# Forced orders where stages hand over, four modulation steps moved, unread matmuls in the routing, and a head scale on VectorE

## The chip, the cores and the metric

The kernel runs on one core of a Trainium2 chip. A core has five engines with a queue of instructions each: TensorE (PE: matmuls, transposes), VectorE (DVE), ScalarE (ACT), GpSimd (POOL) and SyncE (SP, which here only issues DMAs). Each works through its own queue in order; semaphores make one wait for another. The metric is device microseconds (us) of one execution; smaller is better.

## The reference

Two transformer blocks of two layers each, on 256 tokens of width 1024. What matters here is the end of the first block's layers (an mLSTM branch) and the second block.

```python
def _layer(...):                                   # first block, twice
    h_lat = _rms_norm(h_lf + flip(h_lb), g_hd)     # mLSTM heads: 4 of 64, each with its own norm
    y_c = sigmoid(co) * h_lat * silu(cz)
    x = x + gt * (concatenate([y_a, y_b, y_c]) @ w_out)

def second_block(x, c, ...):
    ada_in = silu(c)
    for i in range(2):
        mod = (ada_in @ w_ada[i] + b_ada[i]).reshape(b, 6, d)
        sh_m, sc_m, g_m, sh_f, sc_f, g_f = the six of mod
        hm = rmsnorm(x, norm_mix[i]) * (1 + sc_m) + sh_m
        if i == 0: y = dilated_mixer(hm, ...)
        else:      y = forgetting_mixer(hm, b_w_in, ...)      # FoX
        x = x + g_m * y
        hf = rmsnorm(x, norm_ffn[i]) * (1 + sc_f) + sh_f
        x = x + g_f * hierarchical_moe(hf, ...)
    return x

def hierarchical_moe(h, ...):      # top-1 of 4 groups, then top-2 of 4 experts in it
    ...                            # gates: (tokens, 16), two entries of a row are not zero
    hid = silu(t @ w_gate[e]) * (t @ w_up[e])
    y = sum over e of gates[:, e] * (hid @ w_down[e])
```

## The kernel before

It is written with a framework that keeps one list of instructions for each engine and orders it at build time; tiles come from pools with fixed numbers of buffers (four of `raw`, two of `big`, 1 MB each), and an instruction waits until the buffer that it takes is free. `tc.issue_after(ins)` holds what is issued under it behind `ins` on that engine's list. Tokens are two tiles T of 128; the 1024 columns of a result are two halves n.

The helpers `mm`, `tr`, `act`, `tt`, `ts`, `stt` (lines 281 to 302) issue one instruction each, so most rows of the profile have one of these lines. Matmuls of large weights are done three times in f16, with a weight or activation split in a high and a low part (`wh`, `wl`; `split_w`, line 457: ScalarE makes `wh` from a `raw` tile, VectorE `wl`). `proj` (line 502) is one such projection; between its steps it runs pieces of other work (`settle`, `tick`).

Modulation: `ada` (line 517) is a generator of eight steps for two of the six vectors; a step loads 1 MB of `w_ada` into a `raw` tile and does four fp32 matmuls with 32 output rows (`ps_ad<-raw,cz`; eight records in the trace). `tick(n, a)` takes `a` steps of the queue `adaq`. For layer 1 the vectors of its expert stage ("nf") are queued in `run2` (line 1428) and taken in FoX.

mLSTM: at the end of a tile `head_rstd` makes the head norm `hr` on GpSimd (line 333), and `head_scale` multiplies `yc` by it, on GpSimd too (line 733); TensorE then transposes `yc`. There are six such tiles.

A layer of the second block: `mixer(i)` (line 1451) does the dilated mixer (i=0) or FoX (i=1) and the output projection. After the last projection of a token tile, `post` (line 1478) adds the residual, squares, takes `rstd2`, transposes x (`x_T`), makes the rows `nhl` in two f16 parts (`split_x`: `hi` on ScalarE; `lo` of T=0 on GpSimd by way of `xn`, of T=1 on VectorE) and runs the `router`: logits by TensorE, a copy `lt`, comparisons `df` and the choice `kb` on VectorE. `place(T)` counts the chosen tokens with a matmul on `kb`, `onehot` makes selection matrices OH, `gather0(T)` gathers the first expert pair's rows with 16 matmuls.

`moe(i)` (line 1955) handles 16 experts in eight pairs P: `gate_up(P)` (16 fp32 matmuls, 32 records), `mt` and `mh` (silu times up; ScalarE and VectorE), two transposes and the copy `mhT`, `down(P, n)` for both halves (with an eviction into `oh`, high part on ScalarE, low on VectorE), and `scatter(P)`, eight f16 matmuls that add the pair's rows to four PSUM banks Y. The loop issues gate_up one pair ahead and scatter one pair behind:

```python
            if P < 7:
                gate_up(P + 1)
            ...                                  # transposes of mh, mhT
            if P:
                scatter(P - 1, range(2))
            ohs[P] = self.k4h("oh")
            for n in range(2):
                down(P, n, hT)
        scatter(7, range(2))
```

Then, for each half and tile, the residual: `rsd` (Y times the gate, VectorE) and an addition to x (GpSimd for n=0, VectorE for n=1). Behind it stands the store of the output in layer 1; in layer 0 the squares, the norm `xn`, and in FoX the transposes of `xn`, their modulation (`nv`) and the first projection. FoX (line 1711) first loads the small gate weights `wfr` and fetches and converts the first unit of `b_w_in` in eight pieces.

## Time and profile before

| | |
|---|---|
| median of three runs | 1301.38 us (1296.94 to 1303.22) |
| the profiled execution | 1301.36 us |
| its span, first to last instruction | 1299.2 us |
| mean granted TensorE clock | 0.978 of full speed |
| busy: PE, DVE, ACT, POOL | 1207.5, 772.2, 628.1, 235.2 us |
| HBM read | 288.80 MB, 224 GB/s over the span |

Stages, in us of the span: first block 0 to 550, dilated mixer to 853, first routing to 885, experts of layer 0 to 1002, handover to 1015, FoX to 1143, second routing to 1176, experts of layer 1 to 1291, last residual and store to 1299. A row of a timeline gives the start and length of one or several alike instructions, and in brackets how long the engine sat idle before and whose result ended that. An fp32 matmul has two records. The granted clock is a share of full speed: TensorE runs at one of two levels, 2.4 and 1.2 GHz, and a stretch's number is their mean.

### The profile page before, as it was taken

What the parts mean: (1) busy time and instruction counts of PE and PEld (TensorE: products, weight loads), DVE (VectorE), ACT (ScalarE), POOL (GpSimd) and SP (SyncE); (2) the same over time, 40 slices, a digit from 0 to 9 for tenths busy, and PEclk for the clock granted to TensorE, in tenths of its full rate; (3) what the DMA queues carried; (4) which work ended last, traced back from release to release, by engine and by line L of the source; (5) the groups of instructions that cost most, each with busy time, mean ns of one, the idle gap of its engine ahead of it and who ended that gap; (6) DMA issues with size and microseconds to landing.
All of it is one profiled execution on the core that took longest, in us unless ns stands there. A gap on an engine that the chain in (4) does not pass through costs nothing. (4 is left out here: it accounts for less than half of the span.)

```text
span 1299.2 us, 21044 instructions
## 1 busy us (share of the span) xinstructions
PE 1207.5 (93%) x8064; PEld 574.7 (44%) x8064; DVE 772.2 (59%) x1787; ACT 628.1 (48%) x1373; POOL 235.2 (18%) x254
## 2 busy tenths in 40 slices
PE   6889999989999999899999999979997899979997
PEld 3434544444444544344555555445432445545432
DVE  3776655685567667866778767754213586654213
ACT  3535554444545545666667776533112556533111
POOL 1112000121230001251353235010000413010000
PEclk9999999999999999999999999989999899979999
DMA  9743456244474474587544455867897686617895
GB/s 364 262 163 130 164 194 223 78 162 149 147 275 145 147 259 155 177 311 306 193 162 163 166 190 197 276 259 262 332 399 320 242 309 227 228 49 277 337 398 201
DMA packets 51133, 292.34 MB, mean 225 GB/s; under 512 B 5962, under 2 KB 6218, under 8 KB 24660
## 3 DMA queue, kind: packets, MB, share of 16 engines
q1 hardware_dynamic: 48292, 281.56, 58.7%
q0 software_dynamic: 2736, 9.39, 2.3%
q8 instruction: 65, 1.06, 0.3%
q14 instruction: 40, 0.33, 0.1%
HBM read 288.80 MB, written 2.13 MB: 224 GB/s over the span
## 5 line engine op out<-in xcount | busy, mean ns | idle before, releaser
L298 PE MATMUL ps_mm<-wh,x 128*128 128x512 f16 (+1 forms) x1120 | 381.0, 379 | 5.3 <-DVE x L717 2.0
L298 PEld LDWEIGHTS <-x 128*128 128x128 f16 (+1 forms) x2344 | 189.6, 98 | 245.6 <-issue 92.7
L298 PE MATMUL ps_mm<-wl,x 128*128 128x512 f16 (+1 forms) x736 | 277.1, 377 | 0.0
L459 DVE SCALAR_TENSOR_TENSOR wl<-raw,wh 128x1024 f16<-128x1024 f32 (+2 forms) x188 | 223.0, 1213 | 58.2 <-ACT wh L282 57.8
L282 ACT ACTIVATE wh<-raw 128x1024 f16<-128x1024 f32 (+2 forms) x188 | 183.1, 1015 | 62.6 <-PE ps_mm L298 56.5
L298 PE MATMUL ps_mm<-wh,y 128*128 128x512 f16 (+1 forms) x480 | 174.5, 376 | 0.5 <-DVE y L285 0.3
L298 PE MATMUL ps_ad<-raw,cz 128*32 128x512 f32 (+1 forms) x640 | 112.3, 577 | 13.9 <-DMA raw<-in_w_ada 13.8
L332 POOL TENSOR_SCALAR hss<-hss 128x8 f32<-128x8 f32 (+2 forms) x58 | 20.8, 359 | 446.8 <-DVE hss L726 433.0
L333 POOL TENSOR_TENSOR hr<-hss,nhalf 128x8 f32<-128x8 f32 (+2 forms) x58 | 90.8, 1566 | 4.8
L298 PEld LDWEIGHTS <-y 128*128 128x128 f16 x560 | 54.0, 100 | 60.6 <-issue 13.8
L293 DVE SCALAR_TENSOR_TENSOR oh<-ps_tr,ka,oh 128x512 f16<-128x512 f32 x32 | 24.0, 751 | 78.9 <-ACT oh L282 78.6
L282 ACT ACTIVATE e<-e,ka 128x128 f32<-128x128 f32 (+1 forms) x128 | 56.6, 443 | 24.5 <-DVE ka L1581 24.5
L302 PE MATMUL ps_tr<-consts,e 128*128 128x128 f32 x352 | 59.3, 280 | 1.3 <-DVE qk L293 0.4
L298 PE MATMUL ps_mm<-wh,big 128*128 128x512 f16 x192 | 58.1, 379 | 0.2 <-DVE big L293 0.2
L302 PEld LDWEIGHTS ps_tr<-consts,e 128*128 128x128 f32 x352 | 40.9, 141 | 29.1 <-issue 5.3
L282 ACT ACTIVATE oh<-ps_tr,ka 128x512 f16<-128x512 f32 x32 | 22.0, 687 | 54.5 <-PE ps_tr L298 54.5
L285 DVE TENSOR_TENSOR e2l<-ps_tr,e2h 128x384 f16<-128x384 f32 x64 | 34.1, 554 | 23.1 <-ACT e2h L282 22.1
L282 ACT ACTIVATE e<-ps_s,mx 128x512 f32<-128x512 f32 (+1 forms) x48 | 29.2, 612 | 34.4 <-DVE mx L1020 34.4
L285 DVE TENSOR_TENSOR el<-ps_tr,eh 128x512 f16<-128x512 f32 (+1 forms) x48 | 28.1, 598 | 27.4 <-ACT eh L282 27.1
L298 PEld LDWEIGHTS ps_ad<-raw,cz 128*32 128x32 f32 x640 | 21.2, 111 | 49.1 <-issue 36.5
L282 ACT ACTIVATE e2h<-ps_tr 128x384 f16<-128x384 f32 x64 | 30.0, 481 | 26.5 <-PE ps_o L298 14.5
L298 PEld LDWEIGHTS <-big 128*128 128x128 f16 x288 | 28.1, 98 | 32.5 <-DVE big L293 0.3
(377 smaller groups left out, 1983.8 us busy)
## 6 DMA issues: line engine op xcount, KB each, us to landing
raw<-in_w_ada SPq DMA_DIRECT2D x48, 1024.0 KB
raw<-in_a_w_in SPq DMA_DIRECT2D x36, 1024.0 KB
x<-in_w_gu SPq DMA_DIRECT2D x64, 512.0 KB
...
```

The costliest lines, as they stand in the source:

```text
L282: return self.nc.scalar.activation(out, in_, func, **kw)
L285: return self.nc.vector.tensor_tensor(out, a, b, op=op)
L293: return self.nc.vector.scalar_tensor_tensor(out, a, s, b, op0=op0, op1=op1)
L298: return self.nc.tensor.matmul(out, lhsT, rhs, start=start, stop=stop, **kw)
L302: return self.nc.tensor.transpose(out, in_, self.C("ident")[:n, :n])
L332: self.nc.gpsimd.tensor_scalar(in_, in_, eps, None, op0=OP.add)
L333: self.nc.gpsimd.tensor_tensor(out, in_, self.nhalf.to_broadcast(list(in_.shape)), op=OP.pow)
L459: (on or self.nc.vector).scalar_tensor_tensor(wl, raw, WS, wh, op0=OP.mult, op1=OP.subtract)
```

## The change

At the end of the mLSTM, `yc` is multiplied on VectorE. In the routing, the low part of the first tile's rows is made on VectorE too; `gather0(0)` moves behind the second tile's router, goes through the high parts first, and is followed by five matmuls whose result nobody reads; seven more stand behind the last projection; the second tile's low part is made behind its one-hot. In the experts, scatter(6) is held behind gate_up(7), one half ahead of the transposes of `mh` and one behind; the residual of half 0 is written between the two halves of scatter(7). In layer 0 the first FoX weight is fetched in P=6 and converted in P=7, four of the eight "nf" modulation steps are held behind scatter(7), with two `raw` and two `big` tiles, and the transposes of FoX's norm are held behind the last of these.

The core of the diff:

```diff
 helpers
     def mm(self, out, lhsT, rhs, start, stop, **kw):
-        return self.nc.tensor.matmul(out, lhsT, rhs, start=start, stop=stop, **kw)
+        i = self.nc.tensor.matmul(out, lhsT, rhs, start=start, stop=stop, **kw)
+        self.last_mm = i.ins
+        return i
+    def warm(self, n):
+        p = self.ps("mm").rearrange("p (a n) -> p a n", a=4)
+        for _ in range(n):
+            self.mm(p, self.identh, self.identh[:, None, :].to_broadcast([128, 4, 128]), True, True)
     def ada(...)
-            raw = self.raw()
+            raw = self.adaraw.popleft()() if self.adaraw else self.raw()
 mLSTM, end of a tile
-            self.head_scale(yc.rearrange("p (h d) -> p h d", d=64), yc.rearrange("p (h d) -> p h d", d=64),
-                            r[:, :, None].to_broadcast([128, 4, 64]), 4)
+            yv = yc.rearrange("p (h d) -> p h d", d=64)
+            self.tt(yv, yv, r[:, :, None].to_broadcast([128, 4, 64]), OP.mult)
 run2
-            else:
-                self.adaq.append(self.ada_feat(1, 1, 3, "nf", st["f", 1]))
 mixer, norm(T)
-            self.mod_T(self.xn[T], mods, xT, T)
+            with self.tc.issue_after(self.ada_last):
+                self.mod_T(self.xn[T], mods, xT, T)
 mixer, post(p, T, n, hf)
             self.resid(self.x[T][:, c], p, gb[n])
+            if hf and T and n:
+                self.warm(7)
...
                         self.place(T)
                         self.onehot(0, T, 0)
-                        yield 0.5
-                        self.gather0(T)
 fox
+        W[0] = self.W0
         wr = self.w1("wfr", (8, 16))
         nc.sync.dma_start(wr.rearrange("p k n -> p (k n)"), self.ap["b_w_f"])
-        W[0] = self.conv(self.fetch(units[0]), 1)
 split_x
-        if T == 0:
-            xn = self.k4("xn")
-            self.nc.gpsimd.tensor_scalar(xn, x, r, None, op0=OP.mult)
-            self.nc.gpsimd.tensor_tensor(lo, xn, hi, op=OP.subtract)
-        else:
-            self.stt(lo, x, r, hi, OP.mult, OP.subtract)
+        if T == 0:
+            self.split_lo(T, r)
+    def split_lo(self, T, r):
+        hi, lo = self.nhl[T]
+        self.stt(lo, self.x[T], r, hi, OP.mult, OP.subtract)
 gather0
-        for k in range(8):
-            for a in range(2):
+        for a in range(2):
+            for k in range(8):
 moe, ahead of the experts
-        self.place(1)
-        self.onehot(0, 1, 0)
+        with tc.issue_after(self.last_mm):
+            self.gather0(0)
+            self.warm(5)
+        with tc.issue_after(self.last_mm):
+            self.place(1)
+        oh = self.onehot(0, 1, 0)
+        with tc.issue_after(oh.ins):
+            self.split_lo(1, self.rx[:, 1:2])
         self.gather0(1)
 moe, scatter
-                        Y[T, n] = self.ps({(0, 0): "s", (0, 1): "s", (1, 0): "o", (1, 1): "ad"}[T, n])
+                        Y[T, n] = self.ps({(0, 0): "ad", (0, 1): "s", (1, 0): "o", (1, 1): "s"}[T, n])
 moe, the loop over P
             if P < 7:
-                gate_up(P + 1)
+                up_last = gate_up(P + 1)
...
+            if P == 7:
+                with tc.issue_after(up_last):
+                    scatter(P - 1, (0,))
             (transposes of mh, copy mhT)
-            if P:
+            if P == 6 and i == 0:
+                raws = self.fetch(ap["b_w_in"][0])
+            if P == 7 and i == 0:
+                self.W0 = self.conv(raws, 1)
+            if P == 7:
+                with tc.issue_after(up_last):
+                    scatter(P - 1, (1,))
+            elif P:
                 scatter(P - 1, range(2))
             (both halves of down(P))
-        scatter(7, range(2))
         self.xn = {}
-        (the residual, for n, for T: resid, square, normed or the store)
+        scatter(7, (0,))
+        close(0)
+        ins = scatter(7, (1,))
+        close(1)
+        if i == 0:
+            self.adaq.append(self.ada_feat(1, 1, 3, "nf", st["f", 1]))
+            self.adaraw.extend([self.raw, self.raw] + 2 * [lambda: self.big(F32, (4, 512))])
+            with tc.issue_after(ins):
+                self.tick(0, 4)
+            self.ada_last = self.last_mm
+        def close(n):
+            for T in range(2):
+                (the same residual for one n: resid, square, normed or the store)
```

What the orders become. TensorE at the end of layer 0: the last matmuls of scatter(7), the norm's transposes, the first projection. Before:

```order
L298 LDWEIGHTS OHT
L298 MATMUL ps_s<-oh,OHT 128x512
L298 LDWEIGHTS OHT
L298 MATMUL ps_ad<-oh,OHT 128x512
L302 MATMUL ps_tr<-consts,xn 128x128 x12
L298 LDWEIGHTS x_10884
L298 MATMUL ps_mm<-wh,x_10884 128x512
```

And now:

```order
L299 LDWEIGHTS OHT
L299 MATMUL ps_s<-oh,OHT 128x512
L299 MATMUL ps_ad<-raw,cz 32x512 x8
L299 MATMUL ps_ad<-big,cz 32x512 x8
L311 MATMUL ps_tr<-consts,xn 128x128 x12
L299 LDWEIGHTS x_10945
L299 MATMUL ps_mm<-wh,x_10945 128x512
```

Two groups of eight fp32 matmuls (four modulation steps) stand between scatter(7) and the transposes.

VectorE at the same place: evictions `oh`, residual products `rsd`, additions to `xin`, FoX weight halves `wl`, the norm's `ss` and `xn`. Before:

```order
L293 SCALAR_TENSOR_TENSOR oh<-ps_tr,ka,oh 128x512 x2
L285 TENSOR_TENSOR rsd<-ps_s,gate 128x512
L285 TENSOR_TENSOR rsd<-ps_o,gate 128x512
L285 TENSOR_TENSOR rsd<-ps_s,gate 128x512
L285 TENSOR_TENSOR rsd<-ps_ad,gate 128x512
L738 TENSOR_TENSOR xin<-xin,rsd 128x512 x2
L459 SCALAR_TENSOR_TENSOR wl<-raw,wh 128x512
L293 SCALAR_TENSOR_TENSOR ss<-ssq 128x1
L459 SCALAR_TENSOR_TENSOR wl<-raw,wh 128x512
L289 TENSOR_SCALAR xn<-xin,rs 128x512
L293 SCALAR_TENSOR_TENSOR ss<-ssq 128x1
L459 SCALAR_TENSOR_TENSOR wl<-raw,wh 128x512
```

Now:

```order
L294 SCALAR_TENSOR_TENSOR oh<-ps_tr,ka,oh 128x512
L468 SCALAR_TENSOR_TENSOR wl<-raw,wh 128x512 x4
L294 SCALAR_TENSOR_TENSOR oh<-ps_tr,ka,oh 128x512
L286 TENSOR_TENSOR rsd<-ps_ad,gate 128x512
L468 SCALAR_TENSOR_TENSOR wl<-raw,wh 128x512 x4
L286 TENSOR_TENSOR rsd<-ps_o,gate 128x512
L286 TENSOR_TENSOR rsd<-ps_s,gate 128x512 x2
L747 TENSOR_TENSOR xin<-xin,rsd 128x512 x2
L294 SCALAR_TENSOR_TENSOR ss<-ssq 128x1
L290 TENSOR_SCALAR xn<-xin,rs 128x512
L294 SCALAR_TENSOR_TENSOR ss<-ssq 128x1
```

The eight `wl` stand among the evictions and products; one product is ahead of the second group, and none is left behind the norm.

VectorE in the first routing: residual products and additions, the router's `lt`, `ka`, `df`, `kb`. Before:

```order
L293 SCALAR_TENSOR_TENSOR ss<-ssq 128x1
L285 TENSOR_TENSOR rsd<-ps_mm,x_9225 128x512
L738 TENSOR_TENSOR xin<-xin,rsd 128x512
L1841 COPY lt<-ps_tr 128x128
L293 SCALAR_TENSOR_TENSOR ka<-ps_tr,ka 128x20
L285 TENSOR_TENSOR df<-ka 128x80
L285 TENSOR_TENSOR df<-df,szb 128x80
L1854 TENSOR_REDUCE ka<-df 128x20
L289 TENSOR_SCALAR ka<-ka 128x4
L285 TENSOR_TENSOR rsd<-ps_mm,x_9225 128x512
L293 SCALAR_TENSOR_TENSOR kb<-ka 128x16
```

Now:

```order
L294 SCALAR_TENSOR_TENSOR nhl<-xin,ka,nhl 128x1024
L286 TENSOR_TENSOR rsd<-ps_mm,x_9225 128x512
L747 TENSOR_TENSOR xin<-xin,rsd 128x512
L1849 COPY lt<-ps_tr 128x128
L294 SCALAR_TENSOR_TENSOR ka<-ps_tr,ka 128x20
L286 TENSOR_TENSOR df<-ka 128x80
L286 TENSOR_TENSOR df<-df,szb 128x80
L286 TENSOR_TENSOR rsd<-ps_mm,x_9225 128x512
L1862 TENSOR_REDUCE ka<-df 128x20
L747 TENSOR_TENSOR xin<-xin,rsd 128x512
L290 TENSOR_SCALAR ka<-ka 128x4
L294 SCALAR_TENSOR_TENSOR kb<-ka 128x16
```

`nhl`, the first tile's low part, now stands behind `ss` and ahead of the second tile's products, and `kb` comes behind both of these products and additions.

TensorE at the last pair's end in layer 1 (`ps_tr` of two numbers are the two halves of down(7), `oh` of the smaller number is pair 6's). Before:

```order
L302 MATMUL ps_tr_13452<-consts_80,mh_13450 128x128 x2
L298 MATMUL ps_tr_13466<-qk_13393,mhT_13455 64x512
L298 MATMUL ps_tr_13473<-qk_13393,mhT_13455 64x512
L298 MATMUL ps_tr_13466<-qk_13395,mhT_13455 64x512
L298 MATMUL ps_tr_13466<-qk_13393,mhT_13455 64x512
L298 MATMUL ps_tr_13466<-qk_13395,mhT_13455 64x512
L298 MATMUL ps_tr_13473<-qk_13395,mhT_13455 64x512
L298 MATMUL ps_tr_13473<-qk_13393,mhT_13455 64x512
L298 MATMUL ps_tr_13473<-qk_13395,mhT_13455 64x512
```

Now:

```order
L299 MATMUL ps_s_12975<-oh_13456,OHT_12769 128x512
L311 MATMUL ps_tr_13480<-consts_80,mh_13474 128x128 x2
L299 LDWEIGHTS OHT_12769
L299 MATMUL ps_s_12975<-oh_13456,OHT_12769 128x512
L299 MATMUL ps_tr_13490<-qk_13417,mhT_13483 64x512
L299 MATMUL ps_tr_13490<-qk_13419,mhT_13483 64x512
L299 MATMUL ps_tr_13490<-qk_13417,mhT_13483 64x512
L299 MATMUL ps_tr_13490<-qk_13419,mhT_13483 64x512
L299 MATMUL ps_tr_13497<-qk_13417,mhT_13483 64x512
L299 MATMUL ps_tr_13497<-qk_13419,mhT_13483 64x512
L299 MATMUL ps_tr_13497<-qk_13417,mhT_13483 64x512
L299 MATMUL ps_tr_13497<-qk_13419,mhT_13483 64x512
```

The halves of down(7) follow each other, and pair 6's scatter stands around the transposes.

## Rows read from the trace of the kernel before

**Rows 1.** page, part 1: busy us, share of the span, instructions of each engine

```profile
PE 1207.5 (93%) x8064; PEld 574.7 (44%) x8064; DVE 772.2 (59%) x1787; ACT 628.1 (48%) x1373; POOL 235.2 (18%) x254
```

**Rows 2.** stretches: PE, PEld, DVE, ACT, POOL busy us (instructions), TensorE clock, DMA, GB/s

```profile
860.00:880.00 20.00, 14.10 (x102) 8.31 (x101) 12.75 (x43) 5.99 (x14) 4.36 (x3) 0.74 0.56 219
1000.00:1020.00 20.00, 10.54 (x40) 5.78 (x39) 15.07 (x27) 16.35 (x40) 8.69 (x8) 0.66 0.55 205
1020.00:1040.00 20.00, 20.00 (x141) 8.46 (x139) 10.38 (x12) 8.57 (x13) 7.12 (x7) 1.00 0.69 257
1280.00:1299.00 19.00, 9.84 (x42) 3.31 (x38) 6.66 (x10) 2.14 (x4) 2.48 (x2) 0.92 0.16 60
```

**Rows 3.** waits of TensorE: us in total, times, longest

```profile
PE ps_tr L302 <- POOL yc L733: 7.4, 5, 2.3
```

**Rows 4.** timeline, end of the kernel: start us, busy us, engine, line, operation, [idle before]

```profile
1274.38 0.61 PE L298 MATMUL ps_s<-oh,OHT 128*128 128x512 f16 x2
...
1276.55 3.22 PE L298 MATMUL ps_mm<-x,wh 128*64 128x512 f32 x13
...
1285.10 0.47 PE L302 MATMUL ps_tr<-consts,mh 128*128 128x128 f32 x2 [1.48 <-DVE mh L293]
1286.05 3.71 PE L298 MATMUL ps_tr<-qk,mhT 128*64 128x512 f32 x16 [0.47 <-ACT mhT L282]
...
1288.90 0.69 ACT L282 ACTIVATE oh<-ps_tr,ka 128x512 f16<-128x512 f32 x1 [2.90 <-PE ps_tr L298]
...
1289.62 1.65 DVE L293 SCALAR_TENSOR_TENSOR oh<-ps_tr,ka,oh 128x512 f16<-128x512 f32 x2 [4.66 <-ACT oh L282]
...
1293.57 2.01 DVE L738 TENSOR_TENSOR xin<-xin,rsd 128x512 f32<-128x512 f32 x2
```

**Rows 5.** timeline of TensorE in the first routing

```profile
865.44 0.17 PE L298 MATMUL ps_tr<-kb 128*128 128x16 f16 x1 [2.33 <-DVE kb L293]
...
867.07 1.91 PE L298 MATMUL ps_s<-OH,nhl 128*128 128x128 f16 x16
...
875.29 5.74 PE L298 MATMUL ps_mm<-raw,wh 128*64 128x512 f32 x16
880.87 3.60 PE L298 MATMUL ps_mm<-raw,wl 128*64 128x512 f32 x16
```

**Rows 6.** timeline at the handover from layer 0 to FoX: PE, ACT, DVE

```profile
1009.17 1.94 PE L302 MATMUL ps_tr<-consts,xn 128*128 128x128 f32 x8 [6.82 <-DVE ss L293]
...
1010.76 1.13 ACT L282 ACTIVATE wh<-raw 128x512 f16<-128x512 f32 x2
...
1012.09 3.22 ACT L282 ACTIVATE nv<-ps_tr,mod,modA 128x128 f32<-128x128 f32 x9
...
1004.01 2.01 DVE L738 TENSOR_TENSOR xin<-xin,rsd 128x512 f32<-128x512 f32 x2
...
1010.53 3.09 DVE L459 SCALAR_TENSOR_TENSOR wl<-raw,wh 128x512 f16<-128x512 f32 x5
```

**Rows 7.** timeline of TensorE in FoX: one of eight modulation steps

```profile
1020.84 1.06 PE L298 MATMUL ps_ad<-raw,cz 128*32 128x512 f32 x8
```

**Rows 8.** DMA view, 980 to 1032 in 40 equal slices of 1.3 us

```profile
GB/s 413 403 422 410 438 435 410 422 416 422 435 416 221 95 13 0 126 284 422 25 0 0 0 0 69 227 422 391 429 435 410 44 6 195 422 435 429 410 416 328
```

**Rows 9.** timeline of GpSimd and VectorE in the first routing

```profile
858.79 2.86 POOL L1897 TENSOR_SCALAR xn<-xin,ka 128x1024 f32<-128x1024 f32 x1
...
862.30 1.66 DVE L285 TENSOR_TENSOR df<-ka 128x80 f32<-128x80 f32 x1
863.99 0.24 DVE L285 TENSOR_TENSOR df<-df,szb 128x80 f32<-128x80 f32 x1
...
870.01 1.28 DVE L293 SCALAR_TENSOR_TENSOR nhl<-xin,ka,nhl 128x1024 f16<-128x1024 f32 x1
```

**Rows 10.** timeline of GpSimd and VectorE in an mLSTM stretch

```profile
504.40 1.88 POOL L333 TENSOR_TENSOR hr<-hss,nhalf 128x4 f32<-128x4 f32 x1
...
505.38 0.41 DVE L285 TENSOR_TENSOR vn<-xc,hr 128x256 f32<-128x256 f32 x1
```

27 lines of the change are left out of this document (14 added, 13 removed).

## Prediction

> **What bounds the kernel now.** First the busy shares: TensorE 1207.5 us of a span of 1299.2 [rows 1]. It is the bound, so a change can only win where TensorE idles, where its granted clock is low, or by taking TensorE work off a stretch that it fills. Second the 20-us stretches [rows 2]: TensorE is busy 20.00 of 20 us from 1020 on, but 14.10 from 860 to 880 (first routing, clock 0.74), 10.54 from 1000 to 1020 (between the two layers, clock 0.66) and 9.84 of the last 19. The second routing (1143 to 1176) looks like the first. Third the list of waits, for the mLSTM head scale `yc`: 7.4 us in five [rows 3]. Then those stretches instruction by instruction. The profiled execution took 1301.36 us, its span is 1299.2, so 2.2 us lie around it; the median of the runs shown is 1301.38, so the sum needs no shift.
>
> **End of the experts, both layers.** Before the last expert pair, TensorE does the eight matmuls of scatter(6) from 1274.38 and starts gate_up(7) only at 1276.55; after gate_up(7) it idles 1.48 us for `mh` and 0.47 for `mhT` [rows 4]. The change puts scatter(6) behind gate_up(7), seven matmuls ahead of the transposes and one behind them. A record of 512 columns at the full clock is 0.22 us (sixteen of gate_up in 3.60, [rows 5]), so seven are 1.55 and one 0.22: the idle covers them to within 0.07 us on the first gap and with 0.25 to spare on the second. gate_up(7) and all behind it starts 2.17 us earlier; I take **2.1**. Then down(7): its two output halves were issued turn by turn, so the first came out at 1288.90, 2.85 us after the start at 1286.05 [rows 4]; now the first is half of 3.71 us, 1.86, and its scatter and one residual product go ahead while the second is evicted. Behind VectorE's last `oh` (end 1291.27) there were four products (to 1293.57, 0.58 each) and two additions (2.01) [rows 4]; now three products, and the additions may miss the two on GpSimd that ran beside them. The second half is no sooner than before, so the saving is one product and a little: **0.7**. At the end of the kernel nothing follows but the stores: 2.8 in all. Bounds: 1.5, if the first-half eviction only shifts the wait, and 3.5, if the additions fall to about half.
>
> **Handover from layer 0 to FoX.** The same rows stand 289.56 us earlier at the end of layer 0 (the two additions at 1004.01 and 1293.57, [rows 4, 6]), so down(7) would start 2.1 earlier there too, near 994.4. But eight half-size conversions of the first FoX weight now stand among the evictions. On VectorE one `wl` is 0.62 us (3.09 for five), on ScalarE one `wh` 0.57 (1.13 for two) [rows 6]. From the first `oh` on, near 997.1, VectorE has two `oh` (1.65), eight `wl` (4.95), four products (2.3) and the first addition (0.7): 9.6 us, to 1006.7, where that addition ended near 1005.0 before. From there to the norm's transposes at 1009.17 it took 4.15 us, in which ScalarE also did two `wh` (1.13) ahead of a square; without these 3.0. So the transposes come at 1009.2 to 1009.7: the 2.1 us and the room are eaten, and that step alone is worth nothing. Its return comes next: before, ScalarE did `xn`, three `wh` and two `kb` before it started `nv` at 1012.09, and VectorE was at five `wl` until 1013.62 [rows 6]. Both are free now, and `nv` can start when the first four transposes are done, half of 1.94 us [rows 6] and a hand-over behind 1009.2 to 1009.7: near 1010.4 to 1011.1. **1.3** earlier; bounds 0 and 3.
>
> The second half of this edit is four modulation steps. Each takes TensorE 1.06 us (eight records, [rows 7]) and stood in FoX's projections from 1020.84 on, where TensorE is full [rows 2]; now they stand behind scatter(7), in the 6.82 us of idle before the transposes [rows 6]. That is **4.2** off the bound, if their tiles have landed, since the transposes are held behind the last of these matmuls on TensorE's queue. Data: the DMA engines move 0.42 MB a us when full, and after 997 they were nearly idle for ten us [rows 8]. Two weight tiles (2.1 MB) and four modulation tiles (4.2 MB) follow the last expert weights; three weight tiles (3.1 MB) were in by 997, so the two are in near 994 and the fourth modulation tile near 1004, its matmuls by 1005.5, four us before the transposes can start. Queues passed: on SP the modulation loads now go ahead of the small FoX gate weights, which wait for TensorE, and two more weight tiles go behind these; those were used only after 1020. Taken: 1.3 + 4.2 = **5.5**, bounds 1 and 8. The clock is low around there (0.66, [rows 2]); I leave it as it is.
>
> **Routing, both layers.** Three edits go together. (a) For the first token tile the low half `lo` leaves GpSimd (2.86 us for `xn`, more behind it) for VectorE, 1.28 us [rows 9]. VectorE runs in order, and the instruction now stands ahead of the next residual product, the copy `lt` and the choice `kb`, all of which TensorE waits for: followed through, about 1 us of TensorE idle on `lt`. Against it, `df` took 1.66 us while GpSimd worked, 0.24 otherwise (the next one of that shape) [rows 9]; that 1.4 comes back. Net for `kb`, by following VectorE's new order through: 0.7 later. (b) Sixteen gather matmuls of the first tile (1.91 us, [rows 5]) leave the place ahead of the second tile's router, so the second choice comes 1.5 to 2.2 sooner, and they fill idle later. (c) Seven and five matmuls that nobody reads: 1.5 and 1.1 us at 0.22, the first in the gap of 2.33 before `kb`'s matmul [rows 5], the second in what else of the stretch's 5.9 idle us [rows 2] lies behind it, about 3. At the low clock (twice as long) they take 3.0 and 2.1, and the first group fills the gap and the 0.7 to the last. What arrives is capped by VectorE's gate chain behind: followed through, at most 2.0 a layer. If the clock falls as before it is a loss of 0.2 to 1.4. I take **0.8** a layer, 1.6 in all, nearer to the gain, since the idle is there and the pieces are known; bounds over both layers: 4.0 gained, 2.8 lost.
>
> What can be gained on top is in the clock: gate_up(0) takes 5.74 us for its first sixteen records and 3.60 for its last [rows 5]; the 2.1 between them come from the low one of the two clock levels (1.2 of 2.4 GHz). The Trainium skill ("TensorE: Matmul & The Clock Gate", Part 1: The HAM clock gate) says that throttled is the default state and activity releases it; by that, matmuls nobody reads would hold the clock, and the time would be that of the clock case below.
>
> **mLSTM head scale.** Six `yc` products go to VectorE, 0.41 us for this shape [rows 10]. TensorE waited 7.4 us in five of them [rows 3], but most of that is the wait for the head norm `hr` on GpSimd, which stays there; what goes is the difference of two engines (0.2 us a piece) and one hand-over. Against it, VectorE now waits for `hr` in order, with `mu` and `num` behind it. **0.5**; bounds 1.2 and -2. A row speaks on contention: `vn`, with both inputs on chip, took 0.41 us inside GpSimd's 1.88 us `hr` [rows 10]. The Trainium skill ("SBUF — State Buffer", Who interferes with whom) has it that a VectorE instruction with two inputs in SBUF blocks while a GpSimd instruction reads SBUF; by the rule each `yc` might lose up to that duration. This row does not show it for `hr`, though `df` in rows 9 does for a large GpSimd operation.
>
> **Sum:** 1301.36 - 2.8 - 5.5 - 1.6 - 0.5 = **1291.0**.
>
> **Rivals.** *The handover gives nothing:* the fourth tile lands after 1009.7, or the conversions hold the residuals longer; each us there is a us of FoX. For: six tiles in a row on one queue, and 9.6 us of VectorE work end to end. Against: four us of slack, [rows 8]. 5.5 becomes 0: 1296.5. *The clock stays up:* the gaps in routing and handover are filled well enough. Gain 2.1 for each gate_up(0) and about 2 in FoX's first products: 1291.0 - 6.2 = 1284.8. For: rows 2 show the low clock where TensorE idles. Against: even so it idles about 3 us of the routing. *The unread matmuls land on the path,* the slower side: the choices are ready when they start, since `df` loses its 1.4 us, and they run at the low clock, 0.43 each: 24 are 10.3 us, hiding behind nothing. 1301.4 - 2.8 - 5.5 - 0.5 + 10.3 = 1302.9. It decides where `kb` comes less than 3.0 us (seven of 0.43) behind the last projection matmul. By my reading it comes 2.33 + 0.7 = 3.0 behind, at the edge, so a part is likelier than the whole. *VectorE blocked at the head scale:* six times up to 1.88 us are 11.3: 1302.3; one row against it. *The change does not do what it says:* the printed order shows each edge in place, so this is only the case that the orders are idle, which is the first rival.
>
> **How the numbers follow.** Forecast 0.55, by the unknown ends of its terms 1286 to 1295; handover nothing 0.20 (1296.5); clock up 0.10 (1284.8); unread on the path 0.10 (1302.9); blocked 0.05 (1302.3). 0.5% is 6.5 us, about what a measurement here can tell: faster is below 1294.9, slower above 1307.9. The forecast lies below save for a tenth of it, the clock case whole, and a tenth of the first rival: 0.50 + 0.10 + 0.02, rounded up to 0.64. Slower needs two rivals at once: 0.06. The rest, 0.30, is the same. The range 1284 to 1300 leaves out the two cases above 1302 and a little below.
>
> **What would show it.** Right: gate_up(7) about 2.1 us sooner with no idle before down(7) but a few tenths; eight modulation records of each of four steps between 1001 and 1006, nothing waiting on their DMA; transposes of `xn` near 1009 less what was gained ahead of them; FoX's projections four steps shorter; the last additions 2.8 us nearer to gate_up(7)'s old place. Routing: idle before `kb`'s place under 1.5 us, `df` at 0.24, the second choice sooner. Wrong: a wait of TensorE on a DMA of `raw` or `big` near 1005; transposes past 1010; a first gate_up(0) half over 6 us; waits on `yc` that have only changed their name.

## The result and the profile after

The changed kernel takes 1279.87 us (median of four runs, 1279.46 to 1288.17), the kernel before 1302.3 on the same chip: a ratio of 0.985, 95 % interval 0.980 to 0.990. The forecast was 1291.0 with a range from 1284 to 1300, so the direction was right and the gain, about 22 us, is twice the forecast 10.4 and outside the range. The profiled execution took 1279.46 us, its span is 1277.7 and its mean granted clock 0.989.

The page of the changed kernel, part 1 (answers rows 1):

```profile
PE 1198.2 (94%) x8088; PEld 572.2 (45%) x8088; DVE 768.6 (60%) x1795; ACT 627.6 (49%) x1373; POOL 223.5 (17%) x244
```

Its stretches, placed at the same work as rows 2: first routing, handover, last 19 us (PE, PEld, DVE, ACT, POOL busy us, TensorE clock, DMA share, GB/s):

```profile
856.00:876.00 20.00, 16.91 (x133) 8.22 (x133) 15.33 (x66) 6.44 (x18) 0.55 (x1) 1.00 0.66 247
992.00:1012.00 20.00, 14.32 (x102) 6.62 (x105) 12.94 (x23) 14.58 (x35) 10.41 (x8) 0.91 0.72 298
...
1258.70:1277.70 19.00, 12.05 (x54) 4.25 (x50) 6.04 (x10) 2.14 (x4) 2.52 (x2) 0.87 0.30 119
```

TensorE has 24 more instructions and is busy 9.3 us less. That can't be work taken off it: the routing runs at 1.00 now instead of 0.74 [rows 2], the handover at 0.91 instead of 0.66. Part of the gain is idle time, part is the same matmuls at the higher of the two clock levels. The mean granted clock was 0.978 before and is 0.989 now; with two levels that is about 57 us of the span at the lower one before and 28 now (an estimate: the span times twice what the mean lacks to 1). At the lower level a record of 512 columns starts every 0.43 us instead of 0.22, so at most half of these 29 us, 14.5 of the 21.5, can be matmuls that run faster; the rest is idle time gone.

**Where the time went.** For every ScalarE instruction that a kernel has as often as the kernel before, the shift is its start minus its start there; the median shift around a cut, minus that at the cut ahead, is what a stage gained (-) or lost (us, one profiled execution each). Each line adds up to the difference of the spans, to 0.1. The experiments further down are listed too.

| kernel | first block, mixer | routing 1 | handover | FoX after it | routing 2 | pair 5, layer 1 | end | sum |
|---|---|---|---|---|---|---|---|---|
| forecast | -0.5 | -0.8 | -5.5 with FoX | | -0.8 | 0 | -2.8 | -10.4 |
| changed kernel | -4.3 | -3.45 | -4.9 | -2.6 | -3.2 | +0.9 | -3.9 | -21.5 |
| after_again | -5.9 | -3.45 | -4.9 | -2.6 | -3.2 | +0.9 | -3.9 | -23.0 |
| after_third | -0.2 | -3.45 | -4.4 | -2.6 | -2.7 | +0.9 | -4.0 | -16.5 |
| yc_alone | -3.3 | -1.3 | -0.1 | 0 | 0 | 0 | 0 | -4.6 |
| yc_gpsimd | +0.2 | -3.45 | -3.8 | -2.6 | -1.3 | +2.55 | -4.0 | -12.3 |
| route_back | -4.6 | -0.1 | -4.1 | -2.6 | -0.1 | +2.5 | -3.95 | -12.9 |
| no_unread | -2.8 | -1.9 | -0.5 | -2.6 | -1.4 | +2.6 | -3.9 | -10.5 |
| ada_in_fox | -1.8 | -3.45 | -2.7 | -0.5 | 0 | +2.6 | -4.0 | -9.9 |
| end_alone | -0.5 | -1.3 | -4.15 | -0.7 | -2.7 | +2.55 | -4.0 | -10.7 |
| w0_in_fox | -4.25 | -3.45 | -5.4 | -4.5 | -1.6 | +2.6 | -3.9 | -20.5 |
| w0_in_fox_2 | -4.7 | -3.45 | -5.7 | -4.5 | -3.1 | +0.9 | -4.0 | -24.6 |
| w0_fetch_early | -3.1 | -3.45 | -5.4 | -2.6 | -2.6 | +0.85 | -4.0 | -20.3 |
| unread_alone | +1.6 | -1.9 | -0.2 | 0 | -0.7 | 0 | +0.5 | -0.7 |
| unread_x2 | -4.0 | -0.8 | -4.65 | -2.6 | -0.2 | +2.55 | -4.0 | -13.7 |
| lo_gpsimd | -5.7 | -1.8 | -4.3 | -2.6 | +0.35 | +1.15 | -4.0 | -16.9 |
| branch_late | -3.0 | -3.45 | +1.1 | -2.6 | 0 | +2.55 | -1.55 | -7.0 |

A profiled execution need not be near the median: that of no_unread took 1290.47 us, of branch_late 1294.05 (the slowest of their runs), of ada_in_fox 1291.12. In the changed kernel's profile every term came out on the forecast's side, and every one but the net of the end (3.0) clearly larger; in after_third the first block has no more than 0.2. after_again and after_third are the unchanged new kernel, run again:

> The changed kernel once more, as the yardstick for the three kernels beside it. Both theories: 1279 to 1282 us, ratio to the kernel before 0.983 to 0.988. If single executions land near 1288 again, the scatter of the runs is larger than half of a stage's gain, and stages must be compared by their own lengths in the traces and not by the totals.

Measured: 1280.69 (1277.93 to 1287.72), ratio 0.986 [0.984, 0.988].

> The changed kernel as the yardstick for the two kernels beside it: 1278 to 1282 us.

Measured: 1280.19 (1277.39 to 1284.59), 0.983 [0.981, 0.985]. Between its three profiles the first block differs by 5.7 us, handover and routing 2 by 0.5; routing 1 and the rest of FoX are the same to 0.05. A stage's gain from one profile can be trusted that far and no further, and in routing 2 less, since yc_gpsimd has the same instructions there and gains 1.3.

Two readings stand against each other for the 11 us that the forecast lacks: each edit shortens its own wait by more than was worked out, or the waits are as worked out and the clock, which no longer falls behind them, gives the rest. The first would show as longer idle time gone, the second as the same matmuls in less time. The experiments undo one part, or make one part alone.

### The profile page after: what moved, and what is told of

Its sections match the earlier page's. It is cut to its first block, busy times and chain, and to the rows that moved or that the text cites. A ratio compares the mean times of both kernels' runs of the same rounds, so it can differ in the third digit from the quotient of the medians.

```text
span 1277.7 us, 21080 instructions
## 1 busy us (share of the span) xinstructions
PE 1198.2 (94%) x8088; PEld 572.2 (45%) x8088; DVE 768.6 (60%) x1795; ACT 627.6 (49%) x1373; POOL 223.5 (17%) x244
## 3 DMA queue, kind: packets, MB, share of 16 engines
q8 instruction: 65, 1.06, 0.3%
HBM read 288.80 MB, written 2.13 MB: 228 GB/s over the span
## 5 line engine op out<-in xcount | busy, mean ns | idle before, releaser
L299 PE MATMUL ps_ad<-raw,cz 128*32 128x512 f32 (+1 forms) x624 | 109.3, 578 | 13.5 <-DMA raw<-in_w_ada 13.5
```

Source lines behind the costliest of these rows:

```text
L299: i = self.nc.tensor.matmul(out, lhsT, rhs, start=start, stop=stop, **kw)
```

## Experiments on the head scale

> The kernel before with the one edit that the six head-scale products of the mLSTM run on VectorE. Theory (from the run with that edit undone, 4 to 6 us): the first block ends 4 to 6 us sooner, half of it waits of TensorE on yc (7.4 to about 3.4 us), half the low-clock stretches that these waits caused; total 1295 to 1297. The forecast: 0.5 us, 1300. Rival by the Trainium skill (SBUF, Who interferes with whom), VectorE blocked beside GpSimd: yc takes well over 0.42 us and the total is not better.

The kernel before with this edit alone (shortened: `yc4` and `r4` stand for the views by heads):

```diff
-self.head_scale(yc4, yc4, r4, 4)          # GpSimd
+self.tt(yc4, yc4, r4, OP.mult)            # VectorE
```

1297.11 (1295.08 to 1297.34) beside 1300.57: 0.997 [0.995, 0.998], 3.5 us. Forecast 0.5, upper bound 1.2. TensorE around the first `yc`, in the kernel before (start, us, row, [idle before]):

```profile
237.52 0.44 PE L302 MATMUL ps_tr<-consts,yc 128*128 128x128 f32 x2 [2.13 <-POOL yc L733]
237.80 0.59 PE L298 MATMUL ps_mm<-wl,x 128*128 128x512 f16 x1
238.18 0.63 PE L298 MATMUL ps_mm<-wh,y 128*128 128x512 f16 x1
```

and in yc_alone:

```profile
237.01 0.38 PE L298 MATMUL ps_mm<-wh,x 128*128 128x512 f16 x1
238.64 0.44 PE L302 MATMUL ps_tr<-consts,yc 128*128 128x128 f32 x2 [1.25 <-DVE yc L285]
238.91 0.38 PE L298 MATMUL ps_mm<-wl,x 128*128 128x512 f16 x1
239.13 0.38 PE L298 MATMUL ps_mm<-wh,y 128*128 128x512 f16 x1
```

The stretch from 237 to 245 us, before, then yc_alone:

```profile
237.00:245.00 8.00, 7.41 (x40) 3.70 (x41) 3.94 (x12) 3.35 (x9) 1.74 (x3) 0.79 0.16 68
```

```profile
237.00:245.00 8.00, 5.83 (x46) 3.21 (x46) 5.69 (x19) 3.74 (x10) 2.40 (x3) 1.00 0.29 119
```

Three things. The chain is shorter by what was forecast: from the end of `hr` to the transposes it took 0.74 us before (236.78 to 237.52) and takes 0.51 (238.13 to 238.64). Second, the order was made anew at build time: three more matmuls of 0.22 (0.65 in all) stand ahead of the transposes. 0.23 and 0.65 are the 0.88 by which the wait shrank, and over all pieces 7.4 [rows 3] became this, in the list of waits of the changed kernel:

```profile
PE ps_tr L311 <- DVE yc L286: 3.4, 4, 1.3
```

Third, the matmuls behind the shorter wait start 0.22 apart instead of 0.43, since the clock no longer falls (1.00 against 0.79). Between 225 and 310 us all 13 profiles of kernels with the edit gain 3.2 us, and the three without it 0.1 to 0.65; between 490 and 545 us, around later pieces, the 13 gain 0.9 to 1.85 and the three lose 0.1 to 1.0. One of the three:

> The changed kernel with the head scale of the mLSTM back on GpSimd. Theory: its term was mis-sized, the waits of TensorE on yc go from 3.4 back to 7.4 us and with them come low-clock stretches in the first block: its end (550 us) is 3 to 5 us later, the total too. The forecast's term: 0.5 us. Rival: the 4.3 us by which the first block got shorter are an accident of clock and DMA waits, and the total moves by less than 1 us though the waits on yc come back.

The changed kernel with the lines of that diff the other way round, so the product is on GpSimd again: 1287.74 (1284.1 to 1289.09), 0.989 [0.988, 0.991]. That is 7 us above after_again, on the same chip, by the medians and 4 by the ratios, whose intervals overlap a little. In the first block it has nothing left of the gain (+0.2), but after_third, with the edit, has no more than 0.2 there either, so that column alone settles nothing; 225 to 310 us does. Outside the first block its instructions stand in the same order as the changed kernel's, so the other differences, 1.1 in the handover, 1.9 in routing 2 and 1.7 in pair 5, are no edit at all, and only a part of the 4 to 7 us is the head scale. TensorE in routing 2, first the changed kernel, then yc_gpsimd:

```profile
1143.99 1.05 PE L299 MATMUL ps_s<-OH,nhl 128*128 128x128 f16 x16
1144.88 1.25 PE L299 MATMUL ps_mm<-kb 128*128 128x512 f16 x5
```

```profile
1150.15 1.87 PE L299 MATMUL ps_s<-OH,nhl 128*128 128x128 f16 x16
1151.82 1.85 PE L299 MATMUL ps_mm<-kb 128*128 128x512 f16 x5
```

The rows ahead agree to 0.01 us in length and idle time up to the second tile's logits; from there one is at the lower clock and the other not.

## Experiments on the routing

TensorE, then VectorE, in the first routing of the changed kernel (answers rows 5 and 9):

```profile
859.45 1.69 PE L299 MATMUL ps_mm<-kb 128*128 128x512 f16 x7
861.43 0.17 PE L299 MATMUL ps_tr<-kb 128*128 128x16 f16 x1 [0.29 <-DVE kb L294]
...
863.95 1.06 PE L299 MATMUL ps_s<-OH,nhl 128*128 128x128 f16 x16
864.85 1.25 PE L299 MATMUL ps_mm<-kb 128*128 128x512 f16 x5
...
868.93 3.65 PE L299 MATMUL ps_mm<-raw,wh 128*64 128x512 f32 x16 [0.32 <-ACT wh L283]
```

```profile
859.16 0.24 DVE L286 TENSOR_TENSOR df<-ka 128x80 f32<-128x80 f32 x1
```

The gap ahead of `kb` is 0.29 instead of 2.33 (its matmul comes 1.81 behind the end of the last projection matmul at 859.62, and the unread seven lie in between), `df` takes 0.24 instead of 1.66, the gather runs at the higher clock (1.06 instead of 1.91), and the first half of gate_up(0) takes 3.65 instead of 5.74 [rows 5, 9]: 2.1 us, the price that the clock rival put on it. From the last projection matmul's end to gate_up(0) it is 9.31 us instead of 12.17, 2.9 less. About 1.1 of this is the clock too: in yc_alone, with the old routing, the first gather happened to run at 1.06, and there it is 11.07. In the second routing it is 11.32 instead of 12.62, and the first half of gate_up(0) takes 3.65 instead of 5.21. Of the 2.9 and 2.1 of the first, 3.45 are left at the stage's end: the projection itself ends 0.8 later against the work ahead of it (859.62, shift 3.5 instead of 4.3), and 0.7 go in the first experts.

> The changed kernel with all routing edits undone (low half of the first tile on GpSimd, sixteen gather matmuls ahead of the second router, no unread matmuls); head scale, experts' end and handover as changed. Theory: the routing edits are worth what the traces showed, 2 to 3.5 us a routing with part of it clock, so 4 to 7 us above the changed kernel (1284 to 1287). The forecast's term: 1.6 us for both. Rival: most of the routings' gain in the traces is the phase of the clock, and it is under 2.5 us.

```diff
-                self.warm(7)
 router, behind onehot(0, T, 0)
+                        self.gather0(T)
 split_x, T == 0
-            self.split_lo(T, r)
+            self.nc.gpsimd.tensor_scalar(xn, x, r, None, op0=OP.mult)
+            self.nc.gpsimd.tensor_tensor(lo, xn, hi, op=OP.subtract)
 behind the second router
-        with tc.issue_after(self.last_mm):
-            self.gather0(0)
-            self.warm(5)
 ...
```

All edits of the routing are undone, the gather's order and the second tile's low part too: 1286.19 (1282.12 to 1288.17), 0.988 [0.986, 0.991], above the changed kernel's runs by 5.5 to 6.3 us in the medians and 3 to 6.6 by the ratios, whose intervals overlap in two of the three. Its routings gain 0.1 and 0.1, and the first half of gate_up(0) takes 5.70 again. Against it the edit is worth 3.35 and 3.1 by stage, 6.4 in the two; but yc_alone and end_alone, which have the old routing too, gain 1.3 in routing 1, and end_alone 2.7 in routing 2, so 2.1 to 3.4 in the first and 0.5 to 3.1 in the second is what can be said. Which piece does it?

> The changed kernel without the 24 unread matmuls. Theory: they hold the clock; without them the granted clock falls in both routings as before the change (0.74 to 0.84 of a 20-us stretch), the first half of gate_up(0) takes 5 us or more again instead of 3.65, and each routing is 2 to 2.5 us longer: total 4 to 5 us above the yardstick. Rival A: the new orders alone shorten the routings, the clock stays up or its fall lies beside waiting: within 1 us of the yardstick. Rival B (as forecast for the slower side): part of them lies on the path, so without them it is 1 to 3 us faster.

```diff
-            if hf and T and n:
-                self.warm(7)
...
-            self.warm(5)
```

1285.16 (1284.87 to 1290.47), 0.989 [0.987, 0.990]: 4.5 us above after_again by the medians, 3.4 by the ratios. TensorE in its first routing:

```profile
862.96 0.17 PE L299 MATMUL ps_tr<-kb 128*128 128x16 f16 x1 [1.81 <-DVE kb L294]
...
865.91 1.87 PE L299 MATMUL ps_s<-OH,nhl 128*128 128x128 f16 x16
...
870.87 5.26 PE L299 MATMUL ps_mm<-raw,wh 128*64 128x512 f32 x16
```

The seven lie in a gap that is there without them (1.81), and without them the gather and gate_up(0) are at the lower clock again. By stage they are worth 1.55 and 1.8 us. The 1.55 is outside the scatter, since all nine profiles with the changed routing as it is gain 3.45 there; the 1.8 is not, since yc_gpsimd, with the same instructions in routing 2, gains only 1.3. The total does not tell their worth: the framework's order at the handover came out another way, which cost this kernel 4.4 there.

> The kernel before with seven unread matmuls behind the last projection of each routing (14 in all), orders as before. Theory: they fill 1.5 of the 2.3 us ahead of kb's matmul, but the second router's waits stay, the clock still falls behind them in most executions: 0 to 1.5 us below the kernel before. Rival: the clock is all that the routing edits gain, and seven are enough: 3 to 4 us below.

```diff
             self.resid(self.x[T][:, c], p, gb[n])
+            if hf and T and n:
+                self.warm(7)
```

Added to the kernel before, at this one place: 1299.0 (1296.04 to 1302.59), 0.999 [0.998, 1.000], no difference that can be told. TensorE:

```profile
864.58 1.69 PE L298 MATMUL ps_mm<-kb 128*128 128x512 f16 x7
867.08 0.17 PE L298 MATMUL ps_tr<-kb 128*128 128x16 f16 x1 [0.81 <-DVE kb L293]
...
872.22 0.17 PE L298 MATMUL ps_tr<-kb 128*128 128x16 f16 x1 [0.95 <-DVE ka L293]
...
875.37 5.35 PE L298 MATMUL ps_mm<-raw,wh 128*64 128x512 f32 x16
```

The clock was 1.00 up to gate_up(0) and fell there, behind the idle gaps that the old order leaves. By stage this profile gains 1.9 and 0.7 in the two routings (in the first its gathers run at the higher clock, and gate_up(0) starts 10.63 behind the projection instead of 12.17), but the old routing without unread matmuls gains up to 1.3 and 2.7 in other profiles.

> The changed kernel with 48 instead of 24 unread matmuls (14 and 10 a routing). Theory: the gaps are filled already (0.29 us left ahead of kb's matmul), so the added 12 a routing lie on the path, 0.216 each: 2.6 a routing less about 1 of idle that is left, so 2 to 4 us above the changed kernel. Rival: what matters is the clock, which falls in part of the executions even with 24; twice as many keep it up always, and the median is the same or up to 2 us lower with a smaller scatter.

`warm(14)` and `warm(10)` in place of `warm(7)` and `warm(5)`: 1284.88 (1280.55 to 1287.32), 0.987 [0.986, 0.989], 2 to 5 us above the changed kernel's runs. In routing 1 gate_up(0) starts 11.98 us behind the projection instead of 9.31; 12 more of 0.216 are 2.6, so the start moved by as much as the additional ones take, with the clock at 1.00 in both.

> The changed kernel with the low half of the first token tile back on GpSimd (2.86 + 2.13 us beside VectorE). Theory: the choice kb is held by VectorE's df, which takes 1.7 us again beside GpSimd instead of 0.24, but loses the 1.28 us product ahead of it: net 0 to 1 us a routing, and the clock stays up by the unread matmuls: 0 to 2 us above the changed kernel. Rival: this move is what shortens the routings; then both go back by 2 us or more each, 4 to 6 us above it.

The changed kernel with only the `split_x` part of route_back's diff, `lo` of the first tile on GpSimd: 1284.84 (1284.12 to 1288.39), 0.989 [0.988, 0.990], 4 to 5 us above the changed kernel's runs in the medians and 4 to 7.5 by the ratios. That is nearer the rival (4 to 6) than the theory (0 to 2). Its rows in the first routing, VectorE, then TensorE:

```profile
856.64 1.66 DVE L286 TENSOR_TENSOR df<-ka 128x80 f32<-128x80 f32 x1
```

```profile
859.78 0.17 PE L299 MATMUL ps_tr<-kb 128*128 128x16 f16 x1 [0.81 <-DVE kb L294]
...
867.99 5.35 PE L299 MATMUL ps_mm<-raw,wh 128*64 128x512 f32 x16 [0.33 <-ACT wh L283]
```

`df` is slow again beside GpSimd's large operation, `kb` comes 0.5 later relative to the seven matmuls, and the first half of gate_up(0) takes 5.35, although all the unread matmuls are there. So in these runs neither the orders nor the unread matmuls held the clock by themselves. With both, gate_up(0) took 3.65 in routing 1 in all ten profiles, in routing 2 in seven of the ten.

## Experiments at the handover and the end

TensorE at the handover of the changed kernel (answers rows 6):

```profile
992.77 1.92 PE L299 MATMUL ps_ad<-raw,cz 128*32 128x512 f32 x16
996.11 1.06 PE L299 MATMUL ps_ad<-big,cz 128*32 128x512 f32 x8 [1.42 <-DMA big<-in_w_ada]
998.67 1.06 PE L299 MATMUL ps_ad<-big,cz 128*32 128x512 f32 x8 [1.49 <-DMA big<-in_w_ada]
1000.35 1.06 PE L311 MATMUL ps_tr<-consts,xn 128*128 128x128 f32 x8 [0.62 <-DVE ss L294]
...
1004.30 0.63 PE L299 MATMUL ps_mm<-wh,x 128*128 128x512 f16 x1
```

Its residual additions on VectorE and `nv` on ScalarE:

```profile
996.83 1.81 DVE L747 TENSOR_TENSOR xin<-xin,rsd 128x512 f32<-128x512 f32 x2
...
1001.86 3.58 ACT L283 ACTIVATE nv<-ps_tr,mod,modA 128x128 f32<-128x128 f32 x10
```

All four steps are done by 999.73, two of them behind a wait for their tile (2.9 us), and the transposes still wait 0.62 for the norm. Relative to the work ahead of them (shift 7.8), the transposes come 1.0 sooner and `nv`, at 1001.86, 2.45 sooner than in rows 6. On the time scale of the kernel before, the steps end at 1007.5 (forecast 1005.5) and the transposes start at 1008.1 (forecast 1009.2 to 1009.7).

> The changed kernel with all eight modulation steps of the second expert stage back in FoX; the early conversion of the first FoX weight and the experts' end stay. Theory: 4.2 us of TensorE work come back into FoX, where TensorE is full, and the handover loses the work that kept the clock up, so the transposes and the first products run at the low clock again: 5 to 7 us above the yardstick. Forecast's price: 4.2. Rival: FoX has idle later (1120 to 1140) that takes the steps up: 0 to 2 us.

```diff
 run2
+            else:
+                self.adaq.append(self.ada_feat(1, 1, 3, "nf", st["f", 1]))
 norm(T)
-            with self.tc.issue_after(self.ada_last):
-                self.mod_T(self.xn[T], mods, xT, T)
+            self.mod_T(self.xn[T], mods, xT, T)
 end of moe(0)
 ...
-            with tc.issue_after(ins):
-                self.tick(0, 4)
 ...
```

The four steps are in FoX's queue again, and nothing is held behind them: 1286.46 (1283.81 to 1295.1), 0.990 [0.987, 0.993], 5.8 above after_again, with intervals that overlap. By stage it lacks 4.3 in handover and FoX together, against a forecast of 4.2 for the four steps. It is no clean removal: the framework put sixteen modulation records at the handover anyway, two ahead of the norm's transposes, behind a DMA wait of 4.45 us, and fourteen between their two groups. The other 1.5 is scatter of the first block and routing 2, as in the table.

> The kernel before with the experts' end alone (scatter(6) behind gate_up(7), one output half behind the other, residual of half 0 between the halves of scatter(7)), in both layers; no early weight, no early modulation steps, routing and head scale as before. Theory: 3.1 us at the end of the kernel, and at the end of layer 0 another 2 to 3 that arrive in FoX, since no conversions stand in the way: 1294 to 1296. The forecast's price for this edit at the last residual: 2.8. Rival: at layer 0 the gain waits again for the norm's chain and FoX's weight conversions: 3 us only, 1297.

Of the change only the experts' edits are left; the diffs of yc_gpsimd, route_back, ada_in_fox and w0_in_fox (below) are all made:

```diff
             if P == 7:
                 with tc.issue_after(up_last):
                     scatter(P - 1, (0,))        # stays; (1,) behind the transposes
```

1292.52 (1290.73 to 1295.84), 0.994 [0.993, 0.996], 8 us below 1300.57 (7.4 by the ratio); the theory had 5 to 6. Here the handover gains 4.15 and the end 4.0. (The gain of routing 2 in its line is of the clock, since its instructions there are the old ones.)

> The changed kernel with the first FoX weight fetched and converted in FoX again, behind the modulation tiles; the modulation steps stay early. Theory: the conversions among the evictions cost about 2 us (the forecast's count), so the norm's transposes come 1.5 to 2 us sooner, but the weight lands behind the four modulation tiles and its eight conversions then stand ahead of the first products, which come 2 to 4 us later: 1 to 3 us above the changed kernel. Rival: the weight's conversion hides behind the norm as in the run with the experts' end alone; then 1 to 2 us below the changed kernel.

```diff
-            if P == 6 and i == 0:
-                raws = self.fetch(ap["b_w_in"][0])
-            if P == 7 and i == 0:
-                self.W0 = self.conv(raws, 1)
 fox
-        W[0] = self.W0
 ...
+        W[0] = self.conv(self.fetch(units[0]), 1)
```

The first FoX weight is fetched and converted where it was before, all else as changed: 1276.21 (1274.98 to 1280.48), 0.981 [0.979, 0.984]. Run again beside the changed kernel:

> The first FoX weight fetched and converted in FoX, once more and beside the yardstick. Theory: 3 to 5 us below it, as before (1276): the conversions among the evictions cost more than they give. Rival: chips and phases of the clock made the difference, and it is within 1.5 us.

1276.44 (1275.42 to 1279.72), 0.981 [0.979, 0.983], with after_third at 1280.19: 3.7 us less, in intervals that overlap (0.983 [0.981, 0.985]); by stage 2.4 to 3.2 of it stand in the handover and FoX, the same in both runs. This is the fastest kernel here. TensorE, then VectorE:

```profile
991.82 1.92 PE L299 MATMUL ps_ad<-raw,cz 128*32 128x512 f32 x16
993.56 1.90 PE L299 MATMUL ps_ad<-big,cz 128*32 128x512 f32 x16
996.08 1.06 PE L311 MATMUL ps_tr<-consts,xn 128*128 128x128 f32 x8 [0.62 <-DVE ss L294]
...
1000.68 0.38 PE L299 MATMUL ps_mm<-wh,x 128*128 128x512 f16 x1 [0.91 <-ACT wh L283]
```

```profile
992.95 1.41 DVE L747 TENSOR_TENSOR xin<-xin,rsd 128x512 f32<-128x512 f32 x2
```

No modulation step waits for data, the residual additions end at 994.36 instead of 998.64, and the norm is 4.3 us sooner. The price of a late weight is 0.91 of waiting for `wh` at the first matmul and a little behind it. So the early weight, not the forced order, held the handover back, by the 2.4 to 3.2 us above. By its eight conversions on VectorE, or by its two loads of 1 MB, which stand ahead of the modulation tiles in the DMA queue?

> The changed kernel with the first FoX weight fetched early (in pair 6's turn, ahead of the modulation tiles) and converted in FoX, where the framework places the eight conversions. Theory A (the conversions hold the chain): as fast as with both in FoX, or up to 2 us faster, since the weight is there when the first products need it. Theory B (the loads hold the modulation tiles): TensorE waits about 2.9 us for the modulation tiles again and the gain over the yardstick is lost, within 1 us of it.

```diff
             if P == 6 and i == 0:
-                raws = self.fetch(ap["b_w_in"][0])
+                self.raws0 = self.fetch(ap["b_w_in"][0])
-            if P == 7 and i == 0:
-                self.W0 = self.conv(raws, 1)
 fox
-        W[0] = self.W0
 ...
+        W[0] = self.conv(self.raws0, 1)
```

1280.71 (1275.59 to 1285.08), 0.984 [0.981, 0.987], nothing gained in the totals; handover and FoX together gain 8.0, against 7.5 in the changed kernel and 9.9 in w0_in_fox. TensorE:

```profile
992.89 1.07 PE L299 MATMUL ps_ad<-raw,cz 128*32 128x512 f32 x8 [0.26 <-DMA raw<-in_w_ada]
995.28 1.06 PE L299 MATMUL ps_ad<-raw,cz 128*32 128x512 f32 x8 [1.33 <-DMA raw<-in_w_ada]
997.76 1.93 PE L299 MATMUL ps_ad<-big,cz 128*32 128x512 f32 x8 [1.42 <-DMA big<-in_w_ada]
1000.27 1.94 PE L299 MATMUL ps_ad<-big,cz 128*32 128x512 f32 x8 [0.58 <-DMA big<-in_w_ada]
1002.14 1.97 PE L311 MATMUL ps_tr<-consts,xn 128*128 128x128 f32 x8
```

Now the transposes follow the last modulation matmul at once, and the steps wait 3.6 us for their tiles; the last two also take 1.93 us each, at the lower clock, instead of 1.06. The norm's last `xn` ends at 1000.40 here, ahead of that, although the framework put some conversions among its instructions. So the loads are enough to hold the handover. In the changed kernel the two chains, tiles to modulation and conversions to norm, end within 0.62 us of each other, so taking away one of them shows little; w0_in_fox takes both. That the conversions alone would hold it too, with the tiles in time, was not tried.

**The end of the experts.** TensorE, then VectorE, in layer 1 of the changed kernel (answers rows 4):

```profile
1264.41 0.48 PE L311 MATMUL ps_tr<-consts,mh 128*128 128x128 f32 x2
...
1265.36 3.65 PE L299 MATMUL ps_tr<-qk,mhT 128*64 128x512 f32 x16 [0.26 <-ACT mhT L283]
```

```profile
1272.65 1.39 DVE L747 TENSOR_TENSOR xin<-xin,rsd 128x512 f32<-128x512 f32 x2
```

There is no idle ahead of the transposes and 0.26 ahead of down(7), which starts 3.1 us sooner than the work of pair 6 would have it (1.9 of this is idle: between down(6) and down(7) TensorE stood still for 2.13 before; the other 1.2 lies in records that follow each other more closely, which the forecast did not count); behind it another 0.8 goes (additions 1.39 instead of 2.01). In pair 5 something is given back. TensorE and VectorE there, before and changed:

```profile
1249.64 0.48 PE L302 MATMUL ps_tr<-consts,mh 128*128 128x128 f32 x2 [0.70 <-DVE mh L293]
...
1242.49 0.42 DVE L293 SCALAR_TENSOR_TENSOR mt<-mt,ps_mm 128x256 f32<-128x256 f32 x1 [0.70 <-ACT mt L282]
1249.07 0.42 DVE L293 SCALAR_TENSOR_TENSOR mh<-mt,ps_mm 128x256 f32<-128x256 f32 x1 [6.16 <-PEq L2129]
```

```profile
1232.14 0.47 PE L311 MATMUL ps_tr<-consts,mh 128*128 128x128 f32 x2 [1.61 <-DVE mh L294]
...
1231.12 0.42 DVE L294 SCALAR_TENSOR_TENSOR mt<-mt,ps_mm 128x256 f32<-128x256 f32 x1 [7.75 <-ACT mt L283]
1231.57 0.42 DVE L294 SCALAR_TENSOR_TENSOR mh<-mt,ps_mm 128x256 f32<-128x256 f32 x1
```

A branch for experts with too many tokens stands in the program there, and all engines pass it together. Before, `mt` of the next pair stood ahead of it and only `mh` behind; now both stand behind (ScalarE's half of `mt` waits 8.12 for the branch first), and TensorE waits 0.9 longer. Where the clock falls in that gap, down takes 5.35 instead of 3.65 (yc_gpsimd, at 1240.64), which makes 0.9 into 2.55.

> The changed kernel with the branch for overflowing experts (and the gate loads behind it) at the end of pair 4's turn and not at its start. In all runs with the new experts' end, pair 5 of layer 1 lost 0.9 us or, with the clock fallen, 2.6 us where TensorE waits 1.6 us for mh, which now stands behind the branch. Theory: with scatter, down and gate_up around it the branch hides, and the 0.9 to 2.6 us come back: 1 to 3 us below the changed kernel. Rival: the branch costs the same wherever it stands: same.

```diff
-            if P == 4:
-                self.overflow(i, cnt, CAP)
-                gb = [self.gate_bc(st["g", i][i, 5, 0], n) for n in range(2)]
             p = up.pop(P)
             ...
+            if P == 4:
+                self.overflow(i, cnt, CAP)
+                gb = [self.gate_bc(st["g", i][i, 5, 0], n) for n in range(2)]
             if P < 6:
                 self.moe_dn(i, P + 2)
```

The branch stands at the end of that turn of the loop, behind `mt`, `mh` and down: 1288.51 (1284.43 to 1294.05), 0.990 [0.987, 0.992], 5 to 9 us above the changed kernel's runs. The same 1.62 of waiting for `mh` comes one pair later, with down behind it at 5.25; from pair 5 on the profile is 1.0 behind the kernel before where the changed kernel is 3.1 ahead, and experts and handover of layer 0 lose too (+1.1 instead of -4.9). Code written elsewhere moved the order of a whole stage; this theory fell.

## Why the prediction was too small, step by step

- **What bounds it** was right: TensorE, and only where it idles or is slow. The stages that moved are those that the stretches [rows 2] showed.
- **Head scale: the term that was missed by most.** 0.5 forecast, 1.2 at most; measured 3.5 alone and 4 to 7 when undone in the full change. The step "what goes is the difference of two engines (0.2 us a piece) and one hand-over" has the chain right (0.23) and leaves out that the framework fills the wait with three more matmuls, and that a shorter wait keeps the clock up behind it. The blocking rival did not occur: with the edit `yc` takes VectorE 0.43, and though its wait for `hr` (0.94 in yc_alone's first piece) holds up `mu` and `num`, TensorE runs on without a wait to 243.9. The Trainium skill ("SBUF — State Buffer", Who interferes with whom) says that a VectorE instruction with two inputs in SBUF contends with a GpSimd instruction that reads SBUF. `df` in lo_gpsimd agrees: it takes 1.66, begun beside a large GpSimd operation, and ends 0.1 us behind it (858.30 and 858.21). `vn` [rows 10] was not slowed by a small one, and `yc` can't speak on it, since it waits for `hr` to end. How much of the 4 to 7 is scatter stays open; the 3.5 and the 225 to 310 us are what stands.
- **Routing: most pieces right, the clock left out of the sum.** The gap before `kb` (0.29, forecast under 1.5), `df` (0.24) and the sooner second choice (2.7 us against the work ahead, forecast 1.5 to 2.2) came. "Net for `kb`: 0.7 later" was wrong: its matmul comes 1.81 us behind the last projection matmul, not 3.0, and the seven unread ones fit in since they run at 0.22. The step that failed is the 0.8 a layer, chosen without the clock. In its place the runs show 2.1 to 3.4 in routing 1 and 0.5 to 3.1 in routing 2; in the first, gate_up(0) takes 3.65 instead of 5.74 and starts 2.9 us sooner, partly since the gather ran at the full clock. Without that part the start is 1.75 sooner in routing 1 and 1.3 in routing 2, so the cap of 2.0 on the orders was not shown wrong. The clock rival, given one chance in ten, holds in routing 1 of all ten profiles that have both edits and in routing 2 of seven. "Even so it idles about 3 us" was no argument against it. By the Trainium skill ("TensorE: Matmul & The Clock Gate", Part 1: The HAM clock gate) activity releases the throttle; the trace agrees where the gaps are short too (1.00 in the changed routing), and in unread_alone, where gaps of about 1 us stay, the same seven matmuls did not keep it up for gate_up(0) (5.35). The rival of the unread matmuls on the path did not occur with 12; with 24 the added ones cost 2.6 us in routing 1, at 0.22 each and not at the 0.43 that it charged.
- **Handover: 5.5 forecast, 7.5 measured.** The four steps are worth 4.3 as far as ada_in_fox can tell (4.2). The 1.3 for a sooner `nv` was mis-sized: it was 2.45, since the transposes come 1.0 sooner and not 0 to 0.5 later. The remaining 0.7 may be the clock of FoX's first products (0.54 from 1014 to 1020 us before, 0.73 from 1004 to 1009 now); that is argued, not shown. "Nothing waiting on their DMA" was wrong, 2.9 us are waited there; it was hidden, with 0.62 to spare, by the conversions that the forecast had charged. That the early weight eats what the end of the experts gives was mostly right: the end alone gives 4.15 there, and without the early weight handover and FoX gain 9.9.
- **End: 2.8 forecast, 3.0 measured net.** down(7) 3.1 sooner instead of 2.1 and 0.8 instead of 0.7 behind it; not foreseen was the 0.9 in pair 5.
- **The range** failed since it took the clock as one rival at 6.2 us, priced at both gate_up(0) and FoX's start. It also rose behind a gap that the head scale shortens (0.79 to 1.00), and that term had none of it in the sum. So both readings hold in part: waits shrank by more than was worked out (0.88 at the first `yc`, where 0.23 was the chain), and the clock gave the rest.
